# Two accumulators for the long convolution, the recurrence's functions grouped by table, and a layer norm that ends by token halves

## The chip, the core and the metric

The kernel runs on one core of one Trainium2 chip. A core has TensorE (PE, with its weight loads as PEld), VectorE (DVE), ScalarE (ACT), GpSimd (POOL) and SyncE (SP, which issues most DMAs). The metric is the device time of the program in microseconds (us); lower is better. Times inside a profile are us from the start of the span of one profiled execution. A line such as L468 is line 468 of the kernel file; the lines of the kernel before and of the changed kernel differ by 1 to 29.

## The reference

One decoder layer on 512 tokens of width 1024, all in float32: a feed-forward half-step, a token mixer, a second feed-forward half-step, a final norm.

```python
x = x + 0.5 * swiglu_ffn(rmsnorm(x, ffn1_norm), w_gate1, w_up1, w_down1)      # D_FF = 2816
h = rmsnorm(x, mix_norm)
c_val, c_gate, r_x, r_gate = split(h @ w_in, 4)                               # 512 channels each
u = c_val * sigmoid(c_gate)
u = causal_depthwise_conv(u, conv_dw, conv_dw_bias)                           # 31 taps
u = silu(layernorm(u, conv_ln_g, conv_ln_b))                                  # over the 512 channels
xr = causal_depthwise_conv(r_x, lru_conv_w, lru_conv_b)                       # 4 taps
r, i = sigmoid(block_diag(xr, w_a) + b_a), sigmoid(block_diag(xr, w_x) + b_x)
log_a = -8 * r * softplus(-lam)
a = exp(log_a);  b = sqrt(-expm1(2 * log_a)) * (i * xr)
h_t = a_t * h_(t-1) + b_t                                                     # over the tokens
x = x + concat([u, h * gelu(r_gate)]) @ w_out
x = x + 0.5 * swiglu_ffn(rmsnorm(x, ffn2_norm), w_gate2, w_up2, w_down2)
y = rmsnorm(x, final_norm)
```

## The kernel before

Each float32 matrix product is made of three products of float32r parts (hi x hi, hi x lo, lo x hi), so weights and activations are split into a rounded part and a rest. Products of 512 channels or tokens go into PSUM, which has eight banks of 128 x 512; every tile that `bank` hands out is one of them. In the mixer, channels lie on the partitions and tokens run along the row. Each of the four channel groups (c_val, c_gate, r_x, r_gate) has four channel tiles c = 0 to 3 of 128 x 512.

The layer is a list of units (`Unit`): a product on TensorE and what takes its result out of PSUM. `run` writes them in order and, after each unit with work, calls `step`, which advances the `chains` (generators for norms, the recurrence `lru`, the layer norm) by one step each, and writes taps of the long convolution as long as a rough clock kept in the program lets VectorE or GpSimd keep up with TensorE. A scheduler then orders the instructions on each engine by priority and by what they need; on the chip each engine runs its own list in order and waits on semaphores.

The mixer's units come in this order: c_gate and c_val of tiles 0 and 1 (`zc_units`, by token halves), of tile 2, the four r_x units (`rx_units`), c_gate and c_val of tile 3, the four r_gate units (`rg_units`), then the output projection (`out_units`). The parts that the change touches:

- The long convolution takes the tile `ub` (the 512 tokens and 30 zeros before them). `conv_dve` does it on VectorE: one multiply and add into an accumulator `pc` in PSUM for each tap, L465 for the first and L468 for the others, the last tap writing `cv`. `conv_pool` does one channel tile on GpSimd: ScalarE scales copies (`cm`, L486) and GpSimd adds them up (`ca`, L488). Tile 0 goes to GpSimd, tiles 1 to 3 to VectorE. When a tile is done, `channel_sum` adds its channels with a product with ones (`pm`, L452), and after the fourth the layer norm starts.
- The recurrence `lru` makes gates with block-diagonal products `pga` and Sigmoid (L575, L576), multiplies on GpSimd (L579), takes Tanh (L583) and Exp (L584), the Square of the latter (L588), one VectorE step (L589), Sqrt (L594), a GpSimd product (L595), a scan over the tokens (L600), the product with the GeLU branch `gl` (L609), and splits the result into `yhi` and `ylo` (L610, L611).
- The GeLU of an r_gate unit (L559) is written when its product is done.
- The layer norm subtracts the mean (L500), squares (L505), sums again, takes a root (L509), a reciprocal (L510), and then for each channel tile multiplies (L517), applies Silu (L518) and splits into `uhi` and `ulo` (L519, L520).
- The output projection has 96 passes with y and 96 with u; four token tiles with two halves of the width each (`po`, L336 to L338), added to the residual by `add_res` (L342). After a token tile, its norm for the second feed-forward step begins (L245, L255, transposes `ptr` L269), whose first products are `pgate` and `pup` (L236).

A ScalarE function needs its table loaded; the compiler puts an ACT_TABLE_LOAD ahead of a function that the loaded table lacks.

Of the kernel before, what the change touches and what calls it, by code (L numbers as in the profile page):

```python
# [8 lines left out]
F32 = mybir.dt.float32  # L9
# [9 lines left out]
T = 512  # L19
# [13 lines left out]
PR_SIDE = -400  # L33
RMS_EPS = 1e-6
# [20 lines left out]
def layer_kernel(ctx: ExitStack, tc, x, gains, w_g1, w_u1, w_d1a, w_d1b, w_in,  # L55
# [121 lines left out]
    def run(units):  # L177
# [8 lines left out]
        for i, u in enumerate(units):  # L186
# [21 lines left out]
            clock["pe"] += u.us  # L208
            if u.us:
                step()  # L210
                for g in sides[:1]:
# [200 lines left out]
    def zc_units(c, parts):  # L412
# [11 lines left out]
        def val_out(t0, n):  # L424
            V.tensor_mul(ub[:, c, 30 + t0:30 + t0 + n], box["v"][:, :n], box["s"][:, :n])
            dve(0.7)
            if t0 + n == T:
                if c == 0:
# [30 lines left out]

    def conv_dve(c):  # L460
        acc, o = bank("pc"), conv_out(c)
        for j in range(TAPS):
            src = ub[:, c, j:j + T]
            if j == 0:
                V.tensor_scalar(out=acc, in0=src, scalar1=par(c, P_DW),  # L465
                                scalar2=par(c, P_DWB), op0=ALU.mult, op1=ALU.add)
            else:
                V.scalar_tensor_tensor(out=o if j == TAPS - 1 else acc, in0=src,  # L468
                                       scalar=par(c, P_DW + j), in1=acc,
                                       op0=ALU.mult, op1=ALU.add)  # L470
            yield 0.69
# [22 lines left out]
    def layernorm():  # L494
# [15 lines left out]
        V.reciprocal(rs, rs)  # L510
        dve(3.5)
# [3 lines left out]
        for c in range(4):  # L515
            v, at = conv_out(c), (c // 2, c % 2)
            V.tensor_mul(v, v, rs)  # L517
            S.activation(v, v, AF.Silu, scale=par(c, P_LNG), bias=par(c, P_LNB))  # L518
            S.copy(hi[at[0]][:, at[1], :], v)  # L519
            V.tensor_sub(lo[at[0]][:, at[1], :], v, hi[at[0]][:, at[1], :].bitcast(F32))  # L520
            dve(1.2)
# [29 lines left out]
    def rg_units():  # L551
# [5 lines left out]

        def evac(c):
            S.activation(lr["gl"][c // 2][:, c % 2, :], lr["g", c], AF.Gelu_apprx_tanh)  # L559
# [9 lines left out]
    def lru():  # L569
        xr, r, i_, th = lr["xr"], two("r"), two("i"), two("th")  # L570
        for c in range(4):
# [5 lines left out]
            yield 1  # L577
# [3 lines left out]
        for c in range(4):  # L581
            at = (slice(None), c % 2, slice(None))
            S.activation(th[c // 2][at], r[c // 2][at], AF.Tanh, scale=psp[:, c:c + 1])  # L583
            S.activation(r[c // 2][at], r[c // 2][at], AF.Exp, scale=nsp[:, c:c + 1])  # L584
            if c % 2:
                yield 1
        for q in range(2):
            S.activation(i_[q], r[q], AF.Square)  # L588
            V.scalar_tensor_tensor(out=th[q], in0=i_[q], scalar=1.0, in1=th[q],  # L589
                                   op0=ALU.add, op1=ALU.mult)  # L590
            dve(1.2)
        yield 1
# [4 lines left out]
        yield 1  # L597
        for c in range(4):
            at = (slice(None), c % 2, slice(None))
            V.tensor_tensor_scan(th[c // 2][at], r[c // 2][at], xr[c // 2][at],  # L600
# [242 lines left out]
```

## Time and profile before

| what | value |
|---|---|
| median of 3 runs | 940.53 us (940.41 to 943.63) |
| the profiled execution | 940.52 us, its span 938.3 us, mean granted TensorE clock 0.978 |
| busy in the span | PE 893.9, PEld 741.1, DVE 422.2, ACT 317.9, POOL 90.1 us |
| first feed-forward step | to about 377 us |
| mixer | about 377 to 570 us |
| second feed-forward step and final norm | 570 to 938 us |

A row of a timeline gives start, duration, engine, line, operation, out<-in, shapes, how many instructions are merged, and in brackets how long the engine was idle before and what ended that. A merged row's duration runs from the first start to the last end; neighbouring instructions overlap a little, so that the distance of two starts is shorter than a duration. A row of stretches gives busy time of PE, PEld, DVE, ACT and POOL with their instruction counts, the granted TensorE clock (1.00 is full speed), the share of DMA engines and GB/s.

### The profile page before, as it was taken

To read this page: it belongs to the slowest core of one execution; us is meant where nothing else is said; L and a number is where in the kernel's file an instruction comes from. 1 tells how busy PE (TensorE), PEld (TensorE's weight loads), DVE (VectorE), ACT (ScalarE), POOL (GpSimd) and SP (SyncE) were. 2 spreads that over 40 slices of the span, in tenths; PEclk is the share of its full clock that TensorE was granted. 3 is DMA by queue.
4 is the path that set the end of the run, shared out by engine and by line. 5 is a ranking of instruction groups with operands and counts; after the bars stand their busy time and mean duration, and the time that the engine had idled before them with its cause. 6 is when DMAs were issued, how large, how long until landed. Compare 5 with 4: busy or idle time off the path is not lost.

```text
span 938.3 us, 10242 instructions
## 1 busy us (share of the span) xinstructions
PE 893.9 (95%) x4164; PEld 741.1 (79%) x4164; DVE 422.2 (45%) x500; ACT 317.9 (34%) x421; POOL 90.1 (10%) x112
## 2 busy tenths in 40 slices
PE   8999999999999999999929589999999999999996
PEld 6988888888888888987726369888888888888885
DVE  6644445344444323388749664433323333333224
ACT  6534433233333211354560243332221222223113
POOL 2000011000010000186130000000000000000001
PEclk9999999999999999999978799999999999999999
DMA  8566679266665234465350041322322322232202
GB/s 273 191 238 248 231 293 349 99 231 248 238 232 216 90 93 161 169 249 182 134 179 1 0 135 45 136 90 90 102 100 90 104 98 90 94 109 89 93 21 89
DMA packets 36704, 138.90 MB, mean 148 GB/s; under 512 B 5041, under 2 KB 5169, under 8 KB 33970
## 3 DMA queue, kind: packets, MB, share of 16 engines
q1 hardware_dynamic: 29170, 112.04, 34.6%
q0 software_dynamic: 6912, 25.17, 6.8%
q10 hardware_dynamic: 576, 1.05, 0.3%
q8 instruction: 32, 0.52, 0.2%
q14 instruction: 14, 0.11, 0.0%
HBM read 110.98 MB, written 27.26 MB: 147 GB/s over the span
## 4 chain that ended last, share of the span: by engine, by line
PE 90%; DVE 4%; ACT 4%; DMA 1%; issue 1%; SPq 0%; POOL 0%; POOLq 0%; ACTq 0%
PE pgate L236 26%; PE pup L236 26%; PE pz L236 8%; PE pd L338 6%; PE pd L337 6%; PE pd L336 6%; DVE pc L468 2%; PE pdl L337 2%; PE pdl L336 2%; PE pdl L338 2%; PE pm L452 1%; PE ptr L269 1%; PE po L336 1%; PE po L337 1%; PE po L338 1%; DMA raw<-in_w_u 1%
## 5 line engine op out<-in xcount | busy, mean ns | idle before, releaser
L174 DVE TENSOR_TENSOR hl<-raw,hl 128x1024 fp32r<-128x1024 f32 x132 | 161.5, 1225 | 267.4 <-ACT hl L165 267.4
L165 ACT CAST hl<-raw 128x1024 fp32r<-128x1024 f32 x132 | 138.2, 1048 | 291.4 <-PE pup L236 149.3
L236 PE MATMUL pgate<-h_hi,hl 128*128 128x512 f32 (+1 forms) x768 | 177.2, 373 | 0.5 <-ACT h_hi L274 0.5
L236 PE MATMUL pup<-h_hi,hl 128*128 128x512 f32 (+1 forms) x768 | 176.6, 372 | 0.0
L236 PEld LDWEIGHTS pgate<-h_hi,hl 128*128 128x128 f32 x768 | 137.0, 189 | 26.0 <-ACT h_hi L274 1.2
L236 PEld LDWEIGHTS pup<-h_hi,hl 128*128 128x128 f32 x768 | 137.0, 189 | 24.9
L336 PE MATMUL pd<-hl,act 128*128 128x512 f32 x256 | 99.8, 390 | 0.0
L338 PE MATMUL pd<-hl,act 128*128 128x512 f32 x256 | 99.6, 389 | 0.0
L337 PE MATMUL pd<-hl,act 128*128 128x512 f32 x256 | 99.6, 389 | 0.0
L236 PE MATMUL pgate<-h_lo,hl 128*128 128x512 f32 (+1 forms) x384 | 88.2, 371 | 0.0
L236 PE MATMUL pup<-h_lo,hl 128*128 128x512 f32 (+1 forms) x384 | 88.2, 371 | 0.0
L315 DVE TENSOR_TENSOR sg<-pup,sg 128x512 f32<-128x512 f32 (+1 forms) x48 | 31.1, 647 | 110.7 <-PE pup L236 110.7
L236 PEld LDWEIGHTS pup<-h_lo,hl 128*128 128x128 f32 x384 | 68.4, 188 | 12.5
L236 PEld LDWEIGHTS pgate<-h_lo,hl 128*128 128x128 f32 x384 | 68.4, 188 | 12.4
L311 ACT ACTIVATE sg<-pgate 128x512 f32<-128x512 f32 (+1 forms) x48 | 27.0, 563 | 133.6 <-PE pgate L236 133.6
L468 DVE SCALAR_TENSOR_TENSOR pc<-ub,ch,pc 128x512 f32<-128x512 f32 x87 | 65.7, 755 | 2.8
L236 PE MATMUL pz<-h_hi,hl 128*128 128x512 f32 (+1 forms) x320 | 65.8, 354 | 0.0
L236 PEld LDWEIGHTS pz<-h_hi,hl 128*128 128x128 f32 x320 | 52.1, 189 | 9.6 <-issue 2.4
L337 PEld LDWEIGHTS pd<-hl,act 128*128 128x128 f32 x256 | 48.1, 188 | 10.0
L338 PEld LDWEIGHTS pd<-hl,act 128*128 128x128 f32 x256 | 48.1, 188 | 9.9
L336 PEld LDWEIGHTS pd<-hl,act 128*128 128x128 f32 x256 | 48.1, 188 | 9.9
L225 DVE TENSOR_TENSOR slo<-sraw,shi 128x1024 fp32r<-128x1024 f32 x24 | 29.4, 1225 | 22.8 <-ACT shi L224 22.8
(132 smaller groups left out, 803.0 us busy)
## 6 DMA issues: line engine op xcount, KB each, us to landing
raw<-in_w_g SPq DMA_DIRECT2D x44, 512.0 KB, 3.3
raw<-in_w_u SPq DMA_DIRECT2D x44, 512.0 KB, 3.3
hl<-wsi SPq DMA_DIRECT2D x16, 1024.0 KB, 4.8
sraw<-in_w_in SPq DMA_DIRECT2D x16, 512.0 KB, 4.6
wsi<-shi POOLq DMA_DIRECT2D x16, 512.0 KB, 4.4
wsi<-slo POOLq DMA_DIRECT2D x16, 512.0 KB, 4.6
raw<-in_w_d1b SPq DMA_DIRECT2D x12, 512.0 KB, 3.3
raw<-in_w_d2b SPq DMA_DIRECT2D x12, 512.0 KB, 3.3
```

The lines of the kernel that those rows point to most:

```text
L165: S.copy(s.hi, s.raw)
L174: V.tensor_sub(s.lo, s.raw, s.hi.bitcast(F32))
L225: V.tensor_sub(lo, raw, hi.bitcast(F32))
L236: PE.matmul(ps, w[:, k, :], h[:, k, t0:t0 + n], start=(i == 0 and k == 0), stop=(i == 2 and k == KT - 1))
L269: ins = PE.transpose(pt[:, k, :], xs[0][:, (hf * 4 + k) * P:(hf * 4 + k + 1) * P], ident)
L311: S.activation(box["s"][:, :n], box["gate"][:, :n], AF.Silu)
L315: V.tensor_mul(s[:, :n], box["up"][:, :n], s[:, :n])
L336: PE.matmul(ps, ahi, whi, start=first, stop=False)
L337: PE.matmul(ps, ahi, wlo, start=False, stop=False)
L338: PE.matmul(ps, alo, whi, start=False, stop=last)
L452: PE.matmul(ps, ones, v, start=n == 0, stop=n == 3)
L468: V.scalar_tensor_tensor(out=o if j == TAPS - 1 else acc, in0=src, scalar=par(c, P_DW + j), in1=acc, op0=ALU.mult, op1=ALU.add)
```

## The change

1. `run` calls `step` once per 2.72 us of a unit's nominal time, so twice for most units.
2. The GpSimd convolution takes tile 1, VectorE tiles 0, 2 and 3.
3. `conv_dve` uses two accumulators in two PSUM banks, even taps in one, odd taps in the other, and adds them at the end (one more instruction).
4. `lru` writes Tanh of all tiles, then Exp of all, then both Squares; two gate tiles per step; the VectorE step and the scans are pinned in program order, the scans five steps later (`SCAN_LATER`); the product with the GeLU branch comes after all convolutions.
5. The GeLU of the r_gate units is written after the square roots.
6. The layer norm's reciprocal and all that follows is done by token halves, `ulo` last.
7. The u part of the output projection goes over channel tiles for token tiles 0 and 1 together, then token tile by token tile as before.

```diff
+            n = round(u.us / 2.72)
+            for _ in range(n):
+                clock["pe"] += u.us / n
                 step()
...
-                if c == 0:
+                if c == 1:
                     pool_convs.append(conv_pool(c))
...
     def conv_dve(c):
-        acc, o = bank("pc"), conv_out(c)
+        acc, o = [bank("pc"), bank("pc")], conv_out(c)
         for j in range(TAPS):
-            src = ub[:, c, j:j + T]
+            src, to = ub[:, c, j:j + T], acc[j % 2]
...
+            elif j == 1:
+                V.tensor_scalar(out=to, in0=src, scalar1=par(c, P_DW + 1), scalar2=None,
+                                op0=ALU.mult)
             else:
-                V.scalar_tensor_tensor(out=o if j == TAPS - 1 else acc, in0=src,
-                                       scalar=par(c, P_DW + j), in1=acc,
+                V.scalar_tensor_tensor(out=o if j == TAPS - 2 else to, in0=src,
+                                       scalar=par(c, P_DW + j), in1=to,
                                        op0=ALU.mult, op1=ALU.add)
+        V.tensor_add(o, acc[0], o)
...
-        V.reciprocal(rs, rs)
...
+        half = [slice(0, HT), slice(HT, T)]
+        for i, sl in enumerate(half):
+            V.reciprocal(rs[:, sl], rs[:, sl])
+            for c in range(4):
+                v, o = conv_out(c)[:, sl], hi[c // 2][:, c % 2, sl]
+                V.tensor_mul(v, v, rs[:, sl])
+                S.activation(v, v, AF.Silu, scale=par(c, P_LNG), bias=par(c, P_LNB))
+                S.copy(o, v)
+        for i, sl in enumerate(half):
+            for c in range(4):
+                v, o = conv_out(c)[:, sl], hi[c // 2][:, c % 2, sl]
+                V.tensor_sub(lo[c // 2][:, c % 2, sl], v, o.bitcast(F32))
...
         def evac(c):
-            S.activation(lr["gl"][c // 2][:, c % 2, :], lr["g", c], AF.Gelu_apprx_tanh)
+            need("roots")
+            tc.keep_in_program_order(
+                S.activation(lr["gl"][c // 2][:, c % 2, :], lr["g", c], AF.Gelu_apprx_tanh))
...
             S.activation(th[c // 2][at], r[c // 2][at], AF.Tanh, scale=psp[:, c:c + 1])
+        for c in range(4):
+            at = (slice(None), c % 2, slice(None))
             S.activation(r[c // 2][at], r[c // 2][at], AF.Exp, scale=nsp[:, c:c + 1])
...
-            V.scalar_tensor_tensor(out=th[q], in0=i_[q], scalar=1.0, in1=th[q],
-                                   op0=ALU.add, op1=ALU.mult)
+        yield 1
+        for q in range(2):
+            pin(V.scalar_tensor_tensor(out=th[q], in0=i_[q], scalar=1.0, in1=th[q],
+                                       op0=ALU.add, op1=ALU.mult))
...
+        done["roots"] = True
+        for _ in range(SCAN_LATER):
+            yield 1
         for c in range(4):
-            V.tensor_tensor_scan(th[c // 2][at], r[c // 2][at], xr[c // 2][at],
-                                 0.0, ALU.mult, ALU.add)
-        while "gl" not in done:
+            pin(V.tensor_tensor_scan(th[c // 2][at], r[c // 2][at], xr[c // 2][at],
+                                     0.0, ALU.mult, ALU.add))
+        while "gl" not in done or convs:
             yield 1
...
-        out_ += [Unit(su, 2.72, lambda t=t, oh=oh: part(t, su, "u", False, (oh,)),
-                      lambda t=t, oh=oh: fin(t, oh)) for t in range(4) for oh in range(2)]
+        out_ += [Unit(su, 2.72, lambda c=c: part((0, 1), su, "u", False, (c,)),
+                      fin_two if c == 3 else None) for c in range(4)]
+        out_ += [Unit(su, 2.72, lambda t=t, oh=oh: part((t,), su, "u", False, halves=(oh,)),
+                      lambda t=t, oh=oh: fin(t, oh)) for t in (2, 3) for oh in range(2)]
```

How the instructions stand on the engines. VectorE around the end of the recurrence, before (`th` holds the recurrence's values, `pc` an accumulator of the convolution, `cv` its result):

```order
L589 SCALAR_TENSOR_TENSOR th_3295<-i_3293,th_3295 128x1024
L589 SCALAR_TENSOR_TENSOR th_3296<-i_3294,th_3296 128x1024
L600 SCALAR_TENSOR_TENSOR th_3295<-r_3291,xr_3081 128x512 x2
L609 TENSOR_TENSOR th_3295<-th_3295,gl_3358 128x1024
L600 SCALAR_TENSOR_TENSOR th_3296<-r_3292,xr_3082 128x512 x2
L611 TENSOR_TENSOR ylo_3542<-th_3295,yhi_3540 128x1024
L609 TENSOR_TENSOR th_3296<-th_3296,gl_3359 128x1024
L611 TENSOR_TENSOR ylo_3543<-th_3296,yhi_3541 128x1024
L468 SCALAR_TENSOR_TENSOR cv_3308<-ub,ch,pc_3307 128x512
L465 TENSOR_SCALAR pc_3631<-ub,ch 128x512
L468 SCALAR_TENSOR_TENSOR pc_3631<-ub,ch,pc_3631 128x512 x29
L468 SCALAR_TENSOR_TENSOR cv_3308<-ub,ch,pc_3631 128x512
```

The same place in the changed kernel, from the end of tile 2's convolution to tile 3's first taps:

```order
L475 SCALAR_TENSOR_TENSOR pc_3167<-ub,ch,pc_3167 128x512
L479 TENSOR_TENSOR cv_3169<-pc_3167,cv_3169 128x512
L428 TENSOR_TENSOR ub<-pz_3357,sgc_3353 128x512
L611 SCALAR_TENSOR_TENSOR th_3316<-i_3314,th_3316 128x1024
L611 SCALAR_TENSOR_TENSOR th_3317<-i_3315,th_3317 128x1024
L469 TENSOR_SCALAR pc_3472<-ub,ch 128x512
L472 TENSOR_SCALAR pc_3473<-ub,ch 128x512
L475 SCALAR_TENSOR_TENSOR pc_3472<-ub,ch,pc_3472 128x512
L475 SCALAR_TENSOR_TENSOR pc_3473<-ub,ch,pc_3473 128x512
```

Three more pairs of taps follow, then the four scans (L623), then the other 23 taps, and behind the add of the two accumulators the product with the GeLU branch and the mean's subtraction:

```order
L475 SCALAR_TENSOR_TENSOR pc_3472<-ub,ch,pc_3472 128x512
L479 TENSOR_TENSOR cv_3169<-pc_3472,cv_3169 128x512
L630 TENSOR_TENSOR th_3316<-th_3316,gl_3408 128x1024
L632 TENSOR_TENSOR ylo_3586<-th_3316,yhi_3584 128x1024
L509 TENSOR_TENSOR cv_2950<-cv_2950,pm_3165 128x512 x2
L509 TENSOR_TENSOR cv_3169<-cv_3169,pm_3165 128x512 x2
L630 TENSOR_TENSOR th_3317<-th_3317,gl_3409 128x1024
L632 TENSOR_TENSOR ylo_3587<-th_3317,yhi_3585 128x1024
```

Before, tile 2's last tap and the whole of tile 3's convolution stood behind y; now y stands behind both.

ScalarE between the gates and y, before (`gl` is the GeLU branch, `r` and `i` the gates):

```order
L559 ACT_TABLE_LOAD
L559 ACTIVATE gl_3358<-pz_3360 128x512
L583 ACTIVATE th_3295<-r_3291,psp 128x512 x2
L584 ACT_TABLE_LOAD
L584 ACTIVATE r_3291<-r_3291,nsp 128x512
L559 ACT_TABLE_LOAD
L559 ACTIVATE gl_3358<-pz_3399 128x512
L576 ACT_TABLE_LOAD
L576 ACTIVATE r_3292<-pga_3424,ch 128x512
L576 ACTIVATE i_3294<-pga_3427,ch 128x512
L584 ACT_TABLE_LOAD
L584 ACTIVATE r_3291<-r_3291,nsp 128x512
```

and in the changed kernel:

```order
L603 ACTIVATE th_3317<-r_3313,psp 128x512 x2
L606 ACT_TABLE_LOAD
L606 ACTIVATE r_3312<-r_3312,nsp 128x512 x2
L606 ACTIVATE r_3313<-r_3313,nsp 128x512 x2
L608 ACTIVATE i_3314<-r_3312 128x1024
L608 ACTIVATE i_3315<-r_3313 128x1024
L615 ACT_TABLE_LOAD
L615 ACTIVATE th_3316<-th_3316 128x1024
L615 ACTIVATE th_3317<-th_3317 128x1024
L577 ACT_TABLE_LOAD
L577 ACTIVATE gl_3408<-pz_3410 128x512
```

The GeLUs moved behind the roots, and functions of one table stand together. The whole list has 16 table loads before and 10 now.

TensorE at the end of the input projection, before (`pz` an r_gate unit, `pga` gates, `po` the output):

```order
L575 MATMUL pga_3424<-xr_3082,bd 128x512
L575 MATMUL pga_3427<-xr_3082,bd 128x512
L236 MATMUL pz_3438<-h_hi,hl_3317 128x512 x8
L236 MATMUL pz_3438<-h_lo,hl_3317 128x512 x8
L236 MATMUL pz_3438<-h_hi,hl_3317 128x512 x8
L236 MATMUL pz_3477<-h_hi,hl_3356 128x512 x8
L236 MATMUL pz_3477<-h_lo,hl_3356 128x512 x8
L236 MATMUL pz_3477<-h_hi,hl_3356 128x512 x8
L336 MATMUL po_3550<-hl_3397,yhi_3540 128x512
```

and in the changed kernel:

```order
L239 MATMUL pz_3519<-h_hi,hl_3406 128x512 x8
L239 MATMUL pz_3519<-h_lo,hl_3406 128x512 x8
L239 MATMUL pz_3519<-h_hi,hl_3406 128x512 x6
L455 MATMUL pm_3165<-cv_3169,ones 128x512
L239 MATMUL pz_3519<-h_hi,hl_3406 128x512 x2
L455 MATMUL pm_3165<-cv_3169,ones 128x512
L339 MATMUL po_3594<-hl_3443,yhi_3584 128x512
```

The mean's products of tiles 2 and 3 (`pm`) stand ahead of the output's first product now; the eight gate products moved up together ahead of tile 3's c_val unit, and the layer norm's four sums stand among the first output products.

More of the change, by code (lines that the diff above doesn't have):

```diff
@@ L33 @@
 PR_SIDE = -400
+SCAN_LATER = 5
 RMS_EPS = 1e-6
@@ L207, in run @@
                     live -= not s.in_act
-            clock["pe"] += u.us
-            if u.us:
+            n = round(u.us / 2.72)
+            for _ in range(n):
+                clock["pe"] += u.us / n
                 step()
+            if n:
                 for g in sides[:1]:
@@ L576, in lru @@
                 S.activation(to[c // 2][at], pga, AF.Sigmoid, bias=par(c, b))
-            yield 1
+            if c % 2:
+                yield 1
+        pin = tc.keep_in_program_order
         for q in range(2):
```

52 lines of the change are left out of this document (24 added, 28 removed).

## The prediction

> **What bounds the kernel.** I read the page first, then busy time and granted clock by stretches, then TensorE's waits, then each engine's timeline through the mixer (377 to 570 us). All times are us from the start of the span of the profiled execution. From the page, its head and the engines' shares of the chain that ended last:
>
> ```profile
> span 938.3 us, 10242 instructions
> PE 90%; DVE 4%; ACT 4%; DMA 1%; issue 1%; SPq 0%; POOL 0%; POOLq 0%; ACTq 0%
> ```
>
> TensorE is the bound, and what is not TensorE on that chain can only lie where TensorE waits. The stretches (busy time of each engine, then granted clock, DMA share, GB/s) show where:
>
> ```profile
> 476.00:493.00 17.00, 0.03 (x1) 0.00 (x0) 9.00 (x5) 9.86 (x10) 5.49 (x2) 0.64 0.45 163
> 493.00:501.30 8.30, 7.51 (x17) 5.21 (x18) 7.08 (x9) 1.15 (x2) 0.00 (x0) 0.50 0.01 2
> 515.00:524.00 9.00, 0.05 (x1) 0.00 (x0) 8.61 (x12) 0.00 (x0) 0.00 (x0) 0.69 0.00 1
> 524.00:533.00 9.00, 7.33 (x10) 2.75 (x11) 2.60 (x5) 2.36 (x4) 0.00 (x0) 0.55 0.00 0
> 542.40:545.90 3.50, 3.45 (x8) 2.73 (x9) 2.35 (x5) 3.50 (x6) 0.00 (x0) 0.53 0.78 242
> 570.00:938.30 368.30, 361.02 (x1687) 302.75 (x1685) 125.85 (x142) 98.12 (x135) 4.23 (x10) 1.00 0.27 92
> ```
>
> And what TensorE waited for between 365 and 600 us (sum, times, longest):
>
> ```profile
> PE po L336 <- ACT yhi L610: 17.1, 1, 17.1
> PE pm L452 <- DVE cv L468: 9.1, 1, 9.1
> PE po L336 <- ACT uhi L519: 3.4, 1, 3.4
> PE pm L452 <- ACT sq L505: 1.5, 1, 1.5
> PE po L338 <- DVE ylo L611: 0.6, 1, 0.6
> PE ptr L269 <- DVE xn L255: 0.5, 1, 0.5
> ```
>
> So TensorE stands still from 476: for 17.1 us until the recurrence delivers y, 9.1 us until the last convolution is done, and 6.0 us in small waits: 32.2 us. After each long wait the clock is about half: 7.51 us of work at 0.50 lose 3.8 us, 7.33 at 0.55 lose 3.3, 3.45 at 0.53 lose 1.6, 8.7 us together. From 570 on nothing waits at clock 1.00. The change can reach at most these 40.9 us.
>
> **The change, part by part.** The prices come from these rows of VectorE: taps that alternate with an independent instruction, the halves that end inputs c=0 and c=1, the recurrence's steps, and 29 taps in a row on one accumulator.
>
> ```profile
> 396.25 0.42 DVE L425 TENSOR_TENSOR ub<-pz,sgc 128x256 f32<-128x256 f32 x1 [5.40 <-PE pz L236]
> 402.37 0.42 DVE L425 TENSOR_TENSOR ub<-pz,sgc 128x256 f32<-128x256 f32 x1 [5.69 <-ACT cm L486]
> 420.50 0.75 DVE L468 SCALAR_TENSOR_TENSOR pc<-ub,ch,pc 128x512 f32<-128x512 f32 x1
> 421.16 0.75 DVE L538 SCALAR_TENSOR_TENSOR px<-rxb,ch,px 128x512 f32<-128x512 f32 x1
> 436.25 1.55 DVE L538 SCALAR_TENSOR_TENSOR px<-rxb,ch,px 128x512 f32<-128x512 f32 x2 [3.39 <-ACT rxb L536]
> 471.55 1.23 DVE L589 SCALAR_TENSOR_TENSOR th<-i,th 128x1024 f32<-128x1024 f32 x1 [5.37 <-ACT i L588]
> 486.48 2.33 DVE L600 TENSOR_TENSOR_SCAN th<-r,xr 128x512 f32<-128x512 f32 x2
> 495.31 1.22 DVE L609 TENSOR_TENSOR th<-th,gl 128x1024 f32<-128x1024 f32 x1
> 500.41 22.92 DVE L468 SCALAR_TENSOR_TENSOR pc<-ub,ch,pc 128x512 f32<-128x512 f32 x29
> ```
>
> Two accumulators. A tap whose accumulator was written by the instruction just before starts 0.79 us after it (22.92 / 29); alternating with an independent one it starts after 0.66 us (421.16 - 420.50). The change makes all taps alternate, for one add (taken as 0.66) per tile: 31 x 0.79 = 24.5 us become 32 x 0.66 = 21.1. I take 0.66, since the mixed rows are just this case; the upper end is 0.79. The Trainium skill (VectorE: DVE Perf Modes, The DRAIN you can't avoid) says that the next instruction waits until the pipeline has emptied and that chaining without semaphores saves nothing. By that the two accumulators would win nothing and the add would be a loss, the first rival below; the two rows disagree with it by 0.13 us per tap.
>
> Earlier start. VectorE now takes tile c=0, ready at 396.7, instead of c=1, ready at 402.8: 6.1 us of idle become taps. POOL takes c=1 and starts 6 us later. Walking VectorE's new order at 0.66 us per instruction: tile 0 ends at 421 (its last nine taps wait for the z2 input until 413.7). Tile 2's 41 instructions, with the short convolution's among them, are held by the last short-convolution input: 436.25 before, 437.1 now since one product for the mean (0.86, below) stands ahead on TensorE; 21 instructions follow: 451.0. Before, that tile's last tap ran at 498.8, behind the recurrence.
>
> The functions by table. From ScalarE: a Sigmoid, two Tanh, a table load, an Exp, a Square, a cast of y, four Squares of the layer norm.
>
> ```profile
> 457.13 0.69 ACT L576 ACTIVATE r<-pga,ch 128x512 f32<-128x512 f32 x1 [6.59 <-PE pga L575]
> 473.32 1.32 ACT L583 ACTIVATE th<-r,psp 128x512 f32<-128x512 f32 x2
> 474.67 1.28 ACT L584 ACT_TABLE_LOAD   x1
> 475.96 0.72 ACT L584 ACTIVATE r<-r,nsp 128x512 f32<-128x512 f32 x1
> 482.90 1.04 ACT L588 ACTIVATE i<-r 128x1024 f32<-128x1024 f32 x1
> 496.56 1.05 ACT L610 CAST yhi<-th 128x1024 fp32r<-128x1024 f32 x1 [3.46 <-DVE th L609]
> 527.07 2.36 ACT L505 ACTIVATE sq<-cv 128x512 f32<-128x512 f32 x4 [29.46 <-DVE cv L500]
> ```
>
> And TensorE's: the end of the last gate product ahead of the recurrence, two gate products (four passes), one mean product (two passes), the warm output pace, the layer norm's products and the first use of u, the first product after the mixer:
>
> ```profile
> 438.04 1.98 PE L236 MATMUL pz<-h_hi,hl 128*128 128x512 f32 x8
> 439.86 1.88 PE L575 MATMUL pga<-xr,bd 128*128 128x512 f32 x4
> 441.57 1.02 PE L452 MATMUL pm<-cv,ones 128*128 128x512 f32 x2
> 513.58 0.39 PE L337 MATMUL po<-hl,yhi 128*128 128x512 f32 x1
> 513.80 0.39 PE L338 MATMUL po<-hl,ylo 128*128 128x512 f32 x1
> 527.75 5.83 PE L452 MATMUL pm<-sq,ones 128*128 128x512 f32 x8 [1.50 <-ACT sq L505]
> 542.45 0.80 PE L336 MATMUL po<-hl,uhi 128*128 128x512 f32 x1 [3.39 <-ACT uhi L519]
> 569.58 1.20 PE L236 MATMUL pgate<-h_hi,hl 128*128 128x256 f32 x8
> ```
>
> One pass of a gate or mean product takes 0.43 us, a product two, 0.86; a full-speed pass of the others 0.227, a unit of 24 5.44. The gate of z3 ended at 440.0 and now ends at 440.9. All eight gate products follow at once (6.9: 447.7), then z3's value unit: 453.2. ScalarE keeps pace with the products: last Sigmoid done at 448.5, three Tanh left (0.61 apart, 1.9: 450.4), one load (1.28: 451.7), four Exp (2.6: 454.3), two Squares (1.9: 456.2). The load for Sqrt and the two roots follow at once, 456.2 to 459.5 (1.28 and the Squares' duration each), beside VectorE's work. Between the gates and the GeLU's end ScalarE's order has three loads where there were ten. The GeLU waits behind the roots; its four inputs sit in PSUM until 460 to 477, which costs nothing, since y isn't multiplied by it before 483.
>
> Here VectorE waits: z3's input needs 453.2, and the two steps (L611 of the change) stand in fixed order behind it, for Squares at 455.2 and 456.2. So tile 3's taps, queued behind them, start at 457.5 (1.23 per step). Then in VectorE's order: 8 taps to 462.8, four scans (2.33 a pair: 4.6) to 467.4, 23 taps and the add (24 x 0.66 = 15.8) to 483.2. The scans wait for POOL's products with the roots, and the Squares for POOL's products of the gates, which stand behind its convolution:
>
> ```profile
> 400.94 22.30 POOL L488 TENSOR_TENSOR ca<-ca,cm 128x1024 f32<-128x1024 f32 x9 [19.61 <-ACT cm L486]
> 487.79 3.15 POOL L595 TENSOR_TENSOR xr<-xr,th 128x1024 f32<-128x1024 f32 x1 [2.31 <-ACT th L594]
> ```
>
> At 22.30 / 9 = 2.48 us an addition or product, POOL has fourteen and two halves from 408, stands about 3 us at 435 for ScalarE's scaled copies, ends at 448.3, the gate products at 450.7 and 453.2. The second Square comes at 455.2: 2 us of slack. The products with the roots end at 461.0 and 463.5, the scans that need them start at 462.8 and 465.1.
>
> TensorE meanwhile does the four gate-branch units (21.8) and two mean products (1.7) after 453.2: it runs dry at 476.7. It waits for tile 3's mean, done by VectorE at 483.2, and then for y: multiplication 1.22, cast 1.05, hand-overs 0.1 each: 485.6. Idle net of the mean product: about 8.0 us, against 17.1 + 9.1 + 0.6 before. The second half of y comes behind four subtractions of the mean, at 491.6; the first twelve output passes, cold at 0.43, fill the time to 491.0. The cold start costs 2.5 us, as against 8.7. The Trainium skill (TensorE: Matmul & The Clock Gate, The HAM clock gate) puts the cold time after an idle window at about 3.4 us of activity; by that it would be 1.5. The trace had 8.3 us at 0.50 after its long wait, so I keep 2.5.
>
> The four layer-norm Squares (0.59 apart) come from 491.6 to 494.0, their products end at 495.8. Before, it took 533.0 to 542.45, 9.4 us, from that point to the first use of u. The same puts u at 505, a second half perhaps 4 us later; TensorE has 81 passes of y left, to 514.2. So the halves' extra instructions and the second table load (1.28) lie beside output work, and the waits of 3.4 and 1.5 go. Then 96 passes of u and three transposed tiles (21.8 + 2.6) lead to the next layer's first product at 538.6. Before, a token tile's transposes waited 0.5 us although the 5.5 us of the next tile's passes stood between; now token tiles 0 and 1 end at 523.8 and 525.1 and are transposed at 530.6 and 531.5, 6.8 and 6.4 us later, so I let the 0.5 go too.
>
> The step now runs twice per unit: outside the mixer it moves no instruction. SP's loads of the output weights follow buffers that come free earlier; nothing waits.
>
> The sum, two ways: 569.6 - 538.6 = 31.0; or 32.2 + 8.7 less 8.0 idle, 0.6 wait for the second half and 2.5 cold, 29.8. I take 30. The profiled execution took 940.52 us (2.2 beyond its span), the median of the runs is 940.53: 910.5.
>
> **Rivals.**
> The taps win nothing (0.79): tile 3's 32 instructions end 4.2 us later, and all behind them: 914.7. For it the rows of 29; against it the mixed rows. Chance 0.10.
> POOL is late. If its additions take the 3.15 of the row that ran beside a VectorE product, the convolution ends 10 us later, the gate products 11.3; less 2 of slack, 9 more idle on TensorE: 919.5. Against it: nine additions at 2.48 ran while VectorE did taps. Chance 0.10.
> All is hidden, because VectorE gets ahead of ScalarE: no idle and no cold start, 899.6. Against it: the 26 us of VectorE after 457.5, which TensorE covers for only 19. Chance 0.06.
> The time comes back in another place, the layer norm or the norms ahead of the next layer, so that it ends within 0.5% (4.7 us, about what a measurement here can tell): u would have to be 30 us late where it has 5 to spare. 0.03.
> Slower: POOL's convolution, now the later tile and ahead of the gates' products, holds Squares, scans and the last tile. It decides from (30 + 2) / 15 = 2.1 us more per addition, 4.6 each; at 5.2 the time is 950. The longest row of such a tile is 3.15. Chance 0.02.
>
> **How the numbers follow.** My own case (908 to 913, from the two sums and half a microsecond either way on the chain of steps) has the remaining 0.69. The range 902 to 920 holds it, the taps and POOL's case, and half of the hidden one. Faster by over 0.5%: 0.95; same 0.03; slower 0.02.
>
> **What would show it.** Right: taps 0.66 apart throughout; TensorE dry near 477 and po starting near 486; no wait for uhi; three table loads between the gates and the GeLU; the first product after the mixer near 539. Wrong: taps at 0.79; L611 waiting for POOL; clock 0.5 for more than 6 us after po starts; a new TensorE wait at the transposes.

## The result and the profile after

The changed kernel takes 910.83 us (median; 909.95 to 911.56) against 940.54 for the kernel before on the same chip: a ratio of 0.9676, 95% interval 0.9655 to 0.9698. The prediction was 910.5.

The profiled execution took 910.81 us. Its page, head and shares of the chain that ended last:

```profile
span 909.0 us, 10256 instructions
PE 93%; DVE 4%; ACT 2%; DMA 1%; issue 0%; SPq 0%; POOLq 0%; POOL 0%; ACTq 0%
```

TensorE's waits between 365 and 600 us (sum, times, longest), where there were six rows and 32.2 us before:

```profile
PE pm L455 <- DVE cv L479: 7.1, 1, 7.1
PE po L339 <- ACT yhi L631: 1.5, 1, 1.5
```

The stretches of the mixer's end and the rest (busy time of PE, weight loads, VectorE, ScalarE, GpSimd, then clock, DMA share, GB/s):

```profile
440.00:478.00 38.00, 38.00 (x151) 27.90 (x149) 34.20 (x48) 21.53 (x30) 18.81 (x9) 1.00 0.45 161
478.00:487.00 9.00, 1.94 (x3) 0.50 (x2) 8.31 (x12) 1.22 (x2) 0.00 (x0) 0.81 0.81 290
487.00:491.00 4.00, 3.87 (x11) 2.67 (x11) 3.54 (x6) 0.42 (x1) 0.00 (x0) 0.58 0.26 85
541.00:909.00 368.00, 360.72 (x1685) 302.36 (x1683) 125.56 (x142) 97.94 (x134) 4.22 (x10) 1.00 0.27 92
```

One hole is left, at 478 to 487, with one cold stretch behind it; the 368 us after the mixer are as before. The engines' timelines there (start, us, and what ended the idle time before), VectorE first:

```profile
397.65 0.43 DVE L428 TENSOR_TENSOR ub<-pz,sgc 128x256 f32<-128x256 f32 x1 [5.41 <-PE pz L239]
451.58 0.69 DVE L479 TENSOR_TENSOR cv<-pc,cv 128x512 f32<-128x512 f32 x1
454.76 0.69 DVE L428 TENSOR_TENSOR ub<-pz,sgc 128x512 f32<-128x512 f32 x1 [2.50 <-PE pz L239]
456.73 2.36 DVE L611 SCALAR_TENSOR_TENSOR th<-i,th 128x1024 f32<-128x1024 f32 x2 [1.27 <-ACT i L608]
459.01 0.81 DVE L469 TENSOR_SCALAR pc<-ub,ch 128x512 f32<-128x512 f32 x1
464.32 5.03 DVE L623 TENSOR_TENSOR_SCAN th<-r,xr 128x512 f32<-128x512 f32 x4
469.28 13.89 DVE L475 SCALAR_TENSOR_TENSOR pc<-ub,ch,pc 128x512 f32<-128x512 f32 x21
484.52 0.69 DVE L479 TENSOR_TENSOR cv<-pc,cv 128x512 f32<-128x512 f32 x1
```

ScalarE, GpSimd and TensorE:

```profile
449.92 1.95 ACT L603 ACTIVATE th<-r,psp 128x512 f32<-128x512 f32 x3
455.65 2.00 ACT L608 ACTIVATE i<-r 128x1024 f32<-128x1024 f32 x2
486.38 1.04 ACT L631 CAST yhi<-th 128x1024 fp32r<-128x1024 f32 x1 [7.54 <-DVE th L630]
492.24 1.04 ACT L631 CAST yhi<-th 128x1024 fp32r<-128x1024 f32 x1 [4.82 <-DVE th L630]
504.50 0.70 ACT L530 CAST uhi<-cv 128x256 fp32r<-128x256 f32 x2
448.33 1.29 POOL L499 TENSOR_TENSOR cv<-ca 128x512 f32<-128x512 f32 x1
449.58 4.78 POOL L599 TENSOR_TENSOR xr<-xr,i 128x1024 f32<-128x1024 f32 x2
485.27 2.08 PE L455 MATMUL pm<-cv,ones 128*128 128x512 f32 x2 [7.07 <-DVE cv L479]
487.48 0.80 PE L339 MATMUL po<-hl,yhi 128*128 128x512 f32 x1
490.51 0.40 PE L340 MATMUL po<-hl,yhi 128*128 128x512 f32 x1
540.28 1.20 PE L239 MATMUL pgate<-h_hi,hl 128*128 128x256 f32 x8
```

This execution reaches the mixer 1.4 us later than the one before did (its c=0 half at 397.65 against 396.25). Its first gate product starts at 12.34 us instead of 11.92, and the four up products behind it take 1.05 instead of 0.78. That varies between executions: y_ahead2 below is the same code up to z3's input, and has it 1.9 us earlier than the row at 454.76:

```profile
452.88 0.69 DVE L428 TENSOR_TENSOR ub<-pz,sgc 128x512 f32<-128x512 f32 x1 [2.50 <-PE pz L239]
```

So 1.4 is taken off where absolute times are compared. The first product after the mixer then moves from 569.58 to 538.9, by 30.7 us. The start gives 1.4 back, so the spans differ by 29.3; the two executions run 2.2 and 1.8 us beyond their spans and differ by 29.7.

### The profile page after: what moved, and what is told of

Read it like the earlier page. It is cut to its first block, busy times and chain, and to the rows that moved or that the text cites. A ratio compares the mean times of both kernels' runs of the same rounds, so it can differ in the third digit from the quotient of the medians.

```text
span 909.0 us, 10256 instructions
## 1 busy us (share of the span) xinstructions
PE 888.1 (98%) x4164; PEld 738.8 (81%) x4164; DVE 414.3 (46%) x512; ACT 310.8 (34%) x423; POOL 89.9 (10%) x112
## 3 DMA queue, kind: packets, MB, share of 16 engines
q10 hardware_dynamic: 576, 1.05, 0.3%
## 4 chain that ended last, share of the span: by engine, by line
PE 93%; DVE 4%; ACT 2%; DMA 1%; issue 0%; SPq 0%; POOLq 0%; POOL 0%; ACTq 0%
PE pgate L239 27%; PE pup L239 27%; PE pz L239 7%; PE pd L339 6%; PE pd L341 6%; PE pd L340 6%; PE pdl L341 2%; PE pdl L340 2%; PE pdl L339 2%; DVE pc L475 2%; PE po L339 2%; PE po L341 2%; PE po L340 1%; PE ptr L272 1%; DMA raw<-in_w_u 1%; PE pga L593 1%
## 5 line engine op out<-in xcount | busy, mean ns | idle before, releaser
L475 DVE SCALAR_TENSOR_TENSOR pc<-ub,ch,pc 128x512 f32<-128x512 f32 x84 | 56.9, 750 | 0.0
```

The source lines that it names most:

```text
L475: V.scalar_tensor_tensor(out=o if j == TAPS - 2 else to, in0=src, scalar=par(c, P_DW + j), in1=to, op0=ALU.mult, op1=ALU.add)
```

## The experiments

Theory: the mixer's end is one chain, last inputs, ScalarE's functions, VectorE's steps and tile 3, then y, and each part of the change shortens it. Rivals are in the expectations. All edits are to the changed kernel, except two_acc_sb. Medians are of four or five runs. Ratios are to the kernel before, with 95% intervals; one of 0.001 is 0.94 us.

| kernel | median, us | ratio | mixer time, us |
|---|---|---|---|
| the kernel before | 940.54 | 1 | 173.3 |
| the change | 910.83 | 0.9676 (0.9655 to 0.9698) | 142.6 |
| one_acc | 912.47 | 0.9692 (0.9678 to 0.9705) | 145.9 |
| pool0 | 918.32 | 0.9750 (0.9736 to 0.9765) | 149.6 |
| old_lru | 919.57 | 0.9756 (0.9736 to 0.9777) | 151.3 |
| no_pin | 913.25 | 0.9695 (0.9678 to 0.9713) | 145.5 |
| old_ln | 910.80 | 0.9674 (0.9657 to 0.9690) | 143.1 |
| one_acc_pool0 | 921.56 | 0.9792 (0.9771 to 0.9812) | 153.2 |
| old_lru_one_acc | 919.85 | 0.9771 (0.9750 to 0.9792) | 150.9 |
| old_lru_pool0 | 919.24 | 0.9767 (0.9743 to 0.9792) | 152.6 |
| two_acc_sb | 936.74 | 0.9947 (0.9929 to 0.9966) | 171.6 |
| acc_sb | 929.31 | 0.9872 (0.9850 to 0.9894) | 161.9 |
| y_ahead | 905.46 | 0.9620 (0.9605 to 0.9635) | 138.2 |
| y_ahead2 | 903.78 | 0.9595 (0.9578 to 0.9611) | 135.7 |

The mixer time is taken from the one profiled execution of each kernel: from the c=0 half on VectorE (397.65 in the change) to the first product after the mixer (540.28). In the fourteen traces that half starts anywhere from 395.5 to 398.1, and from that product to the end of the span it is 368.7 to 369.2 us in all of them. So in the whole time the start can hide a difference of up to 2.6 us, which the mixer time leaves out. It stands for one execution each, though, and has no interval.

**one_acc**, the accumulators undone:

```diff
-        acc, o = [bank("pc"), bank("pc")], conv_out(c)
+        acc, o = bank("pc"), conv_out(c)
...
-        V.tensor_add(o, acc[0], o)
```

> The changed kernel with one accumulator per VectorE tile again (31 taps in a row on one bank, no add), all else as it is. Theory A (the taps' pace is on the path): a tap starts 0.79 us after the one before it where nothing stands between, against 0.66 in the changed kernel's profile; tile 3 takes 31 x 0.79 = 24.5 us instead of 32 x 0.66 = 21.1, TensorE's wait for tile 3's mean grows from 7.1 us to about 10.5, and the time is 914.2 (3.4 more than 910.8). Tile 2 ends up to 2 us later, which the 2.5 us that VectorE waits for z3 afterwards swallow. Rival B (the taps' pace is the same, the two accumulators win nothing): the add saved gives 0.7 us back, 910.1. By the Trainium skill (VectorE: DVE Perf Modes, The DRAIN you can't avoid) it would be B. Rival C (they win, but the end is set elsewhere): 910.8, with the wait for the mean at 10 us and a shorter wait behind it.

VectorE's timeline, the scans and the taps of tile 3 behind them:

```profile
464.47 4.56 DVE L619 TENSOR_TENSOR_SCAN th<-r,xr 128x512 f32<-128x512 f32 x4
468.95 17.36 DVE L472 SCALAR_TENSOR_TENSOR pc<-ub,ch,pc 128x512 f32<-128x512 f32 x22
```

and TensorE's wait for the mean (sum, times, longest):

```profile
PE pm L455 <- DVE cv L472: 10.1, 2, 9.7
```

17.36 / 22 = 0.79 us per tap against 13.89 / 21 = 0.66: the pace is as theory A says, and B falls, and with it, as it was read there, the rule of the Trainium skill (VectorE: DVE Perf Modes, The DRAIN you can't avoid). The wait for tile 3 grew by 2.6 us, not 3.4. Half a microsecond of the difference lies in the scans, which took 4.56 us here and 5.03 in the changed kernel. The median grew by 1.6 us, which the overlapping intervals don't part from nothing. The two ends of the mixer time here, from the timelines of VectorE and TensorE, do:

```profile
396.29 0.42 DVE L428 TENSOR_TENSOR ub<-pz,sgc 128x256 f32<-128x256 f32 x1 [5.41 <-PE pz L239]
542.19 1.20 PE L239 MATMUL pgate<-h_hi,hl 128*128 128x256 f32 x8
```

This execution began the mixer 1.4 us earlier than the changed kernel's and ended it 1.9 later: 145.9 us against 142.6, or 3.3 more, which is theory A's 3.4.

**pool0**, the earlier start undone (GpSimd takes tile 0, VectorE starts with tile 1):

```diff
-                if c == 1:
+                if c == 0:
                     pool_convs.append(conv_pool(c))
```

> The changed kernel with GpSimd taking channel tile 0, as before, and VectorE starting with tile 1, whose input is 6.1 us later. Theory A (the earlier start is worth most of its 6 us): VectorE is behind by 3 to 4 us when z3 comes, tile 2's last tap and add go behind the scans (which stand behind one tap of tile 3 and wait for GpSimd to 462.5), tile 3's mean is 4 to 5 us later: 914.5 to 916. Rival B (VectorE's idle time, 1.2 us for z2, 1.0 for the short convolution's input, 2.5 for z3 and 1.3 for the Squares, 6.0 in all, swallows the start): 910.8, with those four waits gone.

TensorE's wait for the mean:

```profile
PE pm L455 <- DVE cv L479: 13.8, 2, 13.0
```

and the scans in VectorE's timeline:

```profile
463.68 6.75 DVE L623 TENSOR_TENSOR_SCAN th<-r,xr 128x512 f32<-128x512 f32 x4 [2.78 <-POOL xr L616]
```

Theory A, and more than it priced: 7.5 us slower, 7.0 in mixer time. The waits for the mean are 13.8 us in all against 7.1. VectorE lost the start, and the scans, now behind one tap, waited 2.8 us for GpSimd.

**old_lru**, the grouping and the fixed places undone (the recurrence and GeLU of before), and **no_pin**, the fixed places alone:

```diff
-        pin = tc.keep_in_program_order
+        pin = lambda i: i
```

> The changed kernel with the recurrence and the GeLU of before: ScalarE's functions as the inputs come (nothing grouped, the GeLU not held back, seven table loads instead of three between the gates and the end of the GeLU), VectorE's steps and scans placed by the scheduler, y multiplied as soon as the GeLU is there. Two accumulators, tile 0 for VectorE and the layer norm's halves stay. Theory A (what counts is that the accumulators and the earlier start leave VectorE free for the recurrence and the last tile; the tables lie beside them): VectorE's work behind z3 is the same to about 1 us, tile 3 ends at 484 to 486 as now, and since both products with the GeLU (2 x 1.22) now stand ahead of its last taps, y is ready at about 482 and TensorE waits 4 to 6 us for it instead of 8.6: 907 to 911. Rival B (the grouping is what brought y forward): four more loads at 1.28 us stand on ScalarE's chain, Sqrt and scans come 5 us later, VectorE waits for them, and the time is 916 or more; if the whole of the 17 us wait comes back, 925.

> The changed kernel with the functions grouped by table as now, but the recurrence's steps, scans and products with the GeLU on VectorE not held in place (the GeLU still is). Its order: scans behind one tap of tile 3 instead of eight, th times gl among the taps, both low parts of y behind some twenty taps. With the ungrouped kernel (919.6) this parts the two halves of that edit. Theory A (the tables cost nothing here, VectorE's order does): the scans wait 2 to 3 us for GpSimd's products (462.5), y's first half comes at 473 but its low part only at 487 to 488, so TensorE stands about 9 us with four passes done, and tile 3 ends at 492 instead of 485: 912 to 918. Rival B (grouping is all): as good as the changed kernel, 910 to 911.5. In that case the 8.7 us of the ungrouped kernel belong to the table loads.

old_lru's waits on TensorE:

```profile
PE po L341 <- DVE ylo L627: 6.4, 1, 6.4
PE po L339 <- ACT uhi L530: 3.7, 1, 3.7
PE po L339 <- ACT yhi L626: 3.2, 1, 3.2
PE pm L455 <- ACT sq L514: 1.5, 1, 1.5
```

The time says rival B, the rows say neither theory. y's first half came early (a wait of 3.2, as theory A had it), but TensorE had three passes to do with it: the low part stood on VectorE behind tile 3's last tap and add, 6.4 us more. And u came late, though tile 3 was done at 487.7. The reason stands in TensorE's queue. Here are the row that ends tile 3 on VectorE and TensorE's last products for the mean, in old_lru, then in **old_lru_one_acc** and **old_lru_pool0** (the same with a second edit undone):

```profile
487.00 0.69 DVE L479 TENSOR_TENSOR cv<-pc,cv 128x512 f32<-128x512 f32 x1
506.68 1.02 PE L455 MATMUL pm<-cv,ones 128*128 128x512 f32 x2
```

old_lru_one_acc:

```profile
492.41 0.75 DVE L472 SCALAR_TENSOR_TENSOR cv<-ub,ch,pc 128x512 f32<-128x512 f32 x1
506.39 1.02 PE L455 MATMUL pm<-cv,ones 128*128 128x512 f32 x2
```

old_lru_pool0:

```profile
500.51 0.69 DVE L479 TENSOR_TENSOR cv<-pc,cv 128x512 f32<-128x512 f32 x1
505.84 1.02 PE L455 MATMUL pm<-cv,ones 128*128 128x512 f32 x2
```

> The changed kernel with two edits undone at once: recurrence and GeLU of before (alone 919.6) and one accumulator (alone 912.5). Theory A (the edits are bounds on one chain on VectorE, so slack that hides the one is used up by the other): the pace costs its full 3.4 us behind z3 and up to 2 more ahead of it, 923 to 925. Rival B (the costs add up): 919.6 + 1.6 = 921.2. Rival C (with the tables ungrouped ScalarE is the bound and the pace is hidden): 919.6.

> The changed kernel with two edits undone at once: recurrence and GeLU of before (alone 919.6) and GpSimd on tile 0 (alone 918.3). Rival B (the costs add up): 919.6 + 7.5 = 927.1. Theory A (one chain on VectorE; the start 6.1 us later goes through to tile 3, and to the low part of y, which stands behind tile 3 there): 925.5 to 930. Rival C (the later start is hidden under ScalarE's ungrouped functions): 919.6 to 921.

Both gave rival C: 919.9 and 919.2, the same as old_lru. Tile 3 ends 5.5 and 13.5 us later and next to nothing happens (0.4 less and 1.3 more in mixer time), since its mean product waits behind output passes until 506 anyway. So the start is worth 7.0 us of mixer time with the new recurrence (the accumulators 3.3), and undone alone neither is worth more than 1.3 with the old one. By these rows that is not because ScalarE became the bound, as rival C had it, but because of the place of the mean product in TensorE's order.

no_pin's 913.2 lies in theory A's range; its low part came after 8.4 us of waiting (8.4 <- ylo L632). Its interval overlaps the change's; the mixer time is 2.8 us longer, so the fixed places look worth about that much beyond the grouping, by one execution.

**one_acc_pool0**, two edits undone:

> The changed kernel with two edits undone at once: one accumulator (alone 912.5) and GpSimd on tile 0 (alone 918.3). With tile 0 on GpSimd VectorE has only 1.4 us left before z3's input and 0.4 before the Squares. Theory A (the slack is gone, so the pace counts in tiles 1 and 2 as well): 3 us behind z3 and 1 to 3 ahead of it, 922 to 924.5. Rival B (the costs add up): 918.3 + 1.6 = 919.9.

10.7 us slower than the change: just under theory A's lower end by the time. The single wait grew to 15.5 us. But its premise isn't borne out: in mixer time the pace costs 3.6 us here (153.2 against 149.6) and 3.3 alone, so the two costs add up to within half a microsecond (10.6 against 3.3 + 7.0), as rival B had it, only with a larger price for the pace. The medians of the two alone, which sum to 9.1, had hidden part of that price.

**old_ln**, the layer norm's end and the output units of before:

```diff
-        for i, sl in enumerate(half):
-            V.reciprocal(rs[:, sl], rs[:, sl])
+        V.reciprocal(rs, rs)
...
-        out_ += [Unit(su, 2.72, lambda c=c: part((0, 1), su, "u", False, (c,)),
```

> The changed kernel with the layer norm's end and the output units of before: one reciprocal, products, Silu, cast and subtraction over all 512 tokens, channel tile by channel tile, and the u part of the outputs token tile by token tile. Theory A (the halves are worth nothing once y comes early): u is ready near 510, TensorE still has y passes up to 515, so no wait for u, and what remains is a wait of about 0.5 us at the transposes: 910.8 to 911.5. Rival B (the halves are worth what the waits for u cost before): waits of 3.4 and 0.5 us with a cold start of 1.6 come back, 916.

Theory A: 910.80, and 0.5 us more in mixer time, with a wait of 0.2 at the transposes. The token halves are worth half a microsecond at most here.

**two_acc_sb**, the accumulators alone on the kernel before, the second one in SBUF:

```diff
-        acc, o = bank("pc"), conv_out(c)
+        o = conv_out(c)
+        acc = [bank("pc"), o]
```

> The kernel before with the two accumulators alone (the second one in SBUF, in the output tile, and not in a second PSUM bank); tile 1 still first, the recurrence and the layer norm as before. Its order has half of tile 3's taps ahead of the recurrence on VectorE, where before they stood behind it. Theory A (the taps are on the path to the second long wait only): y still comes at 493 and TensorE still waits 17 us for it; tile 3 ends at about 512 instead of 524, the 9.1 us wait for its mean goes, and u comes at about 530 where it is needed at 523: 7 us of wait for it instead of 3.4. 929 to 932. Rival B (an accumulator in SBUF gives no faster start, or the layer norm's chain takes it all back): 936 to 941. Rival C (y comes earlier too, as VectorE has fewer taps in front): 925 or less.

936.7, rival B in its first half: beside GpSimd's additions the taps into SBUF were not faster but up to three times slower (2.23 us against 0.74), so tile 3 ended at 522.4 and not 512. The kernel says nothing of the accumulators. **acc_sb** puts the same on the changed kernel to see whether that is so:

> The changed kernel with the second accumulator in SBUF (the output tile) and not in a PSUM bank; all else as it is. In the kernel before with two such accumulators the taps into SBUF took 1.96 us in the mean while GpSimd added (14 of them, up to 2.23), those into PSUM 0.74 at the same time, and both 0.74 once GpSimd had stopped. Theory A (a VectorE instruction with all tiles in SBUF waits for GpSimd's running one): between 409 and 448 us VectorE gets some 25 instructions less done than now and is 11 to 17 us late behind z3: 922 to 928. By the Trainium skill (SBUF — State Buffer) the two engines share a pair of ports and one fully blocks the other. Rival B (the slow taps had another cause there, as the place of the input): 910.8 to 912.

From the timelines GpSimd's first additions, and two taps into SBUF, just ahead of their start and just behind it:

```profile
407.87 29.72 POOL L498 TENSOR_TENSOR ca<-ca,cm 128x1024 f32<-128x1024 f32 x11 [26.33 <-ACT cm L496]
407.17 0.74 DVE L476 SCALAR_TENSOR_TENSOR cv<-ub,ch,cv 128x512 f32<-128x512 f32 x1
408.49 2.33 DVE L476 SCALAR_TENSOR_TENSOR cv<-ub,ch,cv 128x512 f32<-128x512 f32 x1
```

VectorE's groups of taps from 398 to 450 us (busy us, mean ns, idle before):

```profile
L476 DVE SCALAR_TENSOR_TENSOR cv<-ub,ch,cv 128x512 f32<-128x512 f32 x21 | 31.4, 1496 | 0.1
L476 DVE SCALAR_TENSOR_TENSOR pc<-ub,ch,pc 128x512 f32<-128x512 f32 x21 | 15.6, 745 | 0.0
```

Theory A, 18.5 us slower than the change, a little past its range. The same tap takes 0.74 us until GpSimd starts and 2.33 after. VectorE takes up z3's input at 469.8 instead of 454.8, with each trace's start taken off 16 us later, within theory A's 11 to 17.

**y_ahead**: y multiplied among tile 3's taps, each half as its GeLU are ready:

```diff
-        while "gl" not in done or convs:
-            yield 1
...
         for q in range(2):
+            while ("gl", q) not in done:
+                yield 1
             pin(V.tensor_mul(th[q], th[q], lr["gl"][q]))
             S.copy(hi[q], th[q])
-            V.tensor_sub(lo[q], th[q], hi[q].bitcast(F32))
...
+            yield 1
+            pin(V.tensor_sub(lo[q], th[q], hi[q].bitcast(F32)))
```

> The changed kernel with y multiplied before the last convolution is done: each half (th times gl) as soon as its two GeLU are there, and its low part a step later, among tile 3's taps instead of behind them; the rest is unchanged. Theory A (what is left of TensorE's idle time is only the order of y behind tile 3 on VectorE): the first half is ready at 472, its low part at 473, the second half at 481.5 and its low part at 485.5, and TensorE goes from the last gate-branch product (478.2) into the output product warm. The waits of 7.1 us for the mean and 1.5 for yhi go, and 1.3 of the cold start: 910.8 - 9.9 = 900.9. Tile 3 ends 4.9 us later (490.1), but the subtractions of the mean stood behind y before too, so u comes at about the same time (505 to 510) and is needed from 505: up to 1 us of a new wait, 901 to 902. Rival B (the layer norm is the next bound): u comes 5 us later, TensorE waits for uhi about 5 us and starts cold: 906 to 908.

905.46, between the theories. TensorE went into the output without a stop, but then (from the timelines of VectorE and TensorE):

```profile
488.20 0.69 DVE L479 TENSOR_TENSOR cv<-pc,cv 128x512 f32<-128x512 f32 x1
493.28 1.02 PE L455 MATMUL pm<-cv,ones 128*128 128x512 f32 x2
```

and in TensorE's waits:

```profile
PE po L339 <- ACT uhi L530: 3.7, 1, 3.7
```

Once more the mean product is late in TensorE's queue, behind 72 output passes, 4.4 us after tile 3. **y_ahead2** issues the second half of token tile 2's passes behind it and those of tile 3 behind the layer norm's sums:

```diff
+        def behind(key, t, halves):
...
+            with tc.issue_after(pm[key, 3].ins):
+                part((t,), sy, "y", True, halves=halves)
...
+        out_ += [Unit(sy, 2.72, lambda: behind("mean", 2, (1,)))]
         out_ += [Unit([], 0.0, lambda: need("var"))]
-        out_ += [Unit(sy, 5.44, lambda: part((3,), sy, "y", True))]
+        out_ += [Unit(sy, 5.44, lambda: behind("var", 3, (0, 1)))]
```

> The kernel with y ahead (905.46 us), and in TensorE's order the last mean product after 60 output passes instead of 72, twelve further passes and then the layer norm's sums behind it. In its profile the last mean product stood behind output passes until 493.3, though tile 3 was done at 488.9; the Squares, Sqrt and u followed late, and TensorE waited 1.5 us for sq and 3.7 for uhi, then ran 5 us at a clock of 0.67. Theory A (the product's place in TensorE's queue is what delays u): it comes at 490.7, u at about 504.7 instead of 508.7 (one cast less stands ahead of the Silu on ScalarE), and is needed at 503: a wait of up to 1.5 us stays, the other 3.7 and most of the cold loss of 1.6 go: 900.5 to 902. Rival B (u is set by VectorE's and ScalarE's own chain): the waits stay, 905.5. Rival C (y goes behind the mean product and is no longer cover): a new wait of 2 to 3 us ahead of the mean product, 903 to 904.

903.78, the time that rival C gave, but without its new wait ahead of the mean product. The one wait of TensorE left:

```profile
PE po L339 <- ACT uhi L530: 2.8, 1, 2.8
```

and ScalarE's casts of the next weights, from its timeline:

```profile
500.60 2.01 ACT L166 CAST hl<-raw 128x1024 fp32r<-128x1024 f32 x2 [3.87 <-PE po L341]
```

The wait for sq went and that for uhi shrank by 0.9, not by the 2.2 or more of theory A: the two casts in the second row stand ahead of the Silu on ScalarE. Its interval overlaps that of y_ahead a little, and its mixer time is 2.5 us shorter; both are clear of the change's. It is the fastest version here, 0.8% below the change by the ratios.

## Why the prediction was right

**Where the time was.** Right. TensorE's waits went from 32.2 to 8.6 us and the long cold starts from three to one; from 541 on nothing moved.

**Taps.** Right: 0.66 apart. The rival of no gain is out. Its price was sound: it put 32 instructions at 0.79, 4.2 us more; one_acc has 31 and took 3.3 more in mixer time, where 31 x 0.79 less 32 x 0.66 is 3.4.

**The chain.** Each step, 1.4 us taken off the trace, beside the forecast: tile 2 done 450.9 (451.0), Tanh done 450.5 (450.4), Squares 456.2 (456.2), first tap of tile 3 457.6 (457.5), GpSimd's products 453.0 (453.2), scans 462.9 to 468.0 (462.8 to 467.4), tile 3 done 483.8 (483.2), TensorE dry 476.8 (476.7), po 486.1 (485.6), second half of y 491.9 (491.6), first casts of u done 503.8 (505), first product after the mixer 538.9 (538.6). What was 0.6 late on tile 3 is the scans: 5.03 us for the four where I took 4.6 from rows with less beside them.

**What is left.** Together 11.5 us against a forecast of 11.1. Idle net of the mean product: 8.4 instead of 8.0 (478.2 to 487.5, less 0.86), since tile 3, and with it y, came half a microsecond late. The mean product was cold as well, 2.08 us where the forecast had 0.86, but that cost nothing: it ended at 487.35, and the cast of y's first half at 487.42. The wait for the second half: 1.5 instead of 0.6. The cold output passes: twelve took 4.4 us where 2.7 is their warm time, a loss of 1.6 instead of 2.5. These last two cancel, and not by luck: the second half of y, cast at 493.3, ends both whatever the clock does, and the passes were done at 491.8. What was mis-sized is the cold time. The forecast let it begin with the first output pass and last through all twelve, by the stretch of 8.3 us after the 17 us wait. Here it began with the mean product, and the clock was back 5.2 us after TensorE's start (485.27 to 490.51). The 3.4 us of the Trainium skill (TensorE: Matmul & The Clock Gate, The HAM clock gate) are too few here, and 8.3 too many.

**The sum.** Of the two ways the walk through the chain, 31.0, came nearer to the measured 30.7 than the account of waits and cold starts, 29.8, and 30 was taken between them. That the whole time then fell within 0.4 us of 910.5 is in part luck: the start, which the forecast takes as fixed, varies by more than that between executions.

**GpSimd.** Right: done at 448.2 (448.3), ahead of the Squares. No sign of the late case.

**The halves of the layer norm.** Right: beside other work, and old_ln shows them worth half a microsecond at most.

**What the prediction did not see.** It gave one sum for the whole chain, and nothing in it says that the pieces don't add. Undone alone, accumulators, start, recurrence and halves cost 1.6, 7.5, 8.7 and 0 by the medians, or 17.8 in all, and 3.3, 7.0, 8.7 and 0.5 in mixer time, or 19.5 of 30.7. And with the old recurrence 21 us of the 29.7 are still there (940.5 to 919.6), where accumulators or start, undone, cost next to nothing. No run undoes both there, or the halves. What brought the 21 us isn't settled by a run. old_lru's trace shows one thing that differs from the kernel before: the last gate products and the last Sigmoid stand much earlier.

In old_lru:

```profile
451.12 3.60 PE L591 MATMUL pga<-xr,bd 128*128 128x512 f32 x8
454.86 0.68 ACT L592 ACTIVATE i<-pga,ch 128x512 f32<-128x512 f32 x1
```

and in the kernel before:

```profile
463.23 1.88 PE L575 MATMUL pga<-xr,bd 128*128 128x512 f32 x4
467.65 0.68 ACT L576 ACTIVATE i<-pga,ch 128x512 f32<-128x512 f32 x1
```

Before there are four groups of four passes and ten table loads up to y; in old_lru two groups of eight and seven loads. The prediction tells the gates' coming together as part of the new recurrence, and said of the step, which now runs twice per unit, only that it moves nothing outside the mixer. In the order of old_lru with one step per unit the gate products stand in four groups again, with nine loads. So the finer step is the likely cause; that is read from orders and was not run.

## What to carry to other kernels

Walk the chain behind the last input engine by engine and in queue order; the steps here came within 0.6 us, u within 1.2. Don't split the sum among the edits: a product that stands too late in one engine's queue makes whatever finishes ahead of it worthless, and y_ahead met the same product 4.4 us late again. Before making a producer faster, look at where its consumer stands in its own queue. And where the start of an execution varies, compare the part of the trace that the edit can reach, and not only whole times: one_acc's 1.6 us by the medians was 3.3 there.

## What the runs showed of the hardware

In acc_sb a VectorE tap with its accumulator and its input both in SBUF takes 0.74 us while GpSimd is idle, 2.33 when it starts to add, and 2.69 once later on (at 449.33), and GpSimd's additions go from 2.48 (27.25 / 11, the row of the changed kernel below) to 2.70 us (29.72 / 11):

```profile
409.09 27.25 POOL L497 TENSOR_TENSOR ca<-ca,cm 128x1024 f32<-128x1024 f32 x11 [26.35 <-ACT cm L495]
```

With the accumulator in PSUM the same tap stays at 0.745 beside the same additions. The Trainium skill (SBUF — State Buffer, SBUF: two separate sides) says so: an operation of VectorE with two SBUF inputs and one of GpSimd that reads SBUF hold a shared pair of ports one at a time. The rows agree: both engines' instructions get longer side by side, and the taps that accumulate in PSUM don't. They show the delay, not the ports. The delay makes the choice of two PSUM banks for the accumulators, and not the free output tile, worth 18.5 us.
